# Input rows of a streaming-encoder step: load point, buffer of the sums of squares, and engine of the adds

## The chip, the core and the metric

One core of a Trainium2 chip runs the whole program. The metric is device time in microseconds (us), median of several executions; lower is better. The kernel before took 3329.35 us (median of 3 runs, 3321.38 to 3330.4). The engines are PE (TensorE, matmuls), PEld (its weight loads), DVE (VectorE), ACT (ScalarE), POOL (GpSimd) and SP (SyncE, which here issues most of the DMAs). Each engine works through its own list of instructions in order, and waits at the head of that list.

## What is computed

One inference step of a one-layer hybrid encoder on 2048 prompt frames, 16 meta tokens and 64 frames of a running stream, 2128 rows in all of 1024 features, in float32. Only its first stage is touched here:

```python
def rms_norm(x, g):
    y = x * rsqrt(mean(x * x, axis=-1) + EPS)
    return y * g

def input_projection(x, pos, lp):
    h = rms_norm(x, lp['attn_norm'])
    z = einsum('bld,dc->blc', h, lp['w_in'])      # 1024 -> 2728 columns
    q_lat, kv_lat, k_rope_raw, qkv, gate, beta_logit, a_logit = split(z)
```

After it come latent attention (8 heads), a gated delta rule with a causal convolution (4 heads), an output projection and a squared-ReLU MLP, each with residuals. They are the same in both kernels.

## The kernel before

The data are held transposed: features on the 128 partitions, rows along the free axis. The first stage, `phase_a`, splits the 2128 rows into five blocks of 336, 512, 512, 512 and 256 rows (`BLOCKS`), and the 2728 columns of the projection into 22 column tiles of 128 (the last, number 21, has 40). The column tiles are worked in batches: first tiles 21, 3 and 4 together, then tiles 5 to 16 singly (the convolution's inputs), then the rest. For each batch all five blocks are gone through. As the split rows of all blocks stay in SBUF, the input rows are loaded only once, in the first batch. This is where the change lies.

Every float32 product is made from three rounded ones: a value is split into a high part (ACT, L134) and a low part (DVE, L135), and PE adds high by high, low by high and high by low (L270, L271, L272). One column tile of one block (`col_product`) is 8 x 3 matmuls into one of six PSUM buffers.

`load_x(b)` takes the eight feature slices of a block's rows: SP issues the DMA of a slice into one of four buffers `x` (L224), ACT rounds it (L134), DVE subtracts (L135), ACT squares it (L227 for the first slice, L230 for the others), and DVE adds the squares up (L231) in the tile `ss`, of which there is one for all blocks (`bufs=1`). `mean_rstd` then sums `ss` over the partitions with a matmul by ones on PE (L241, two records), DVE scales (L243), and the reciprocal root is made on ACT (L141, L142) and DVE (L143 to L146) and put into `rstd[:, block]`, a tile as wide as all rows. `col_finish` multiplies a product by it (DVE, L282 for the tiles of the first batch), which frees the PSUM buffer. `finish_cols` squares the finished tiles 3 and 4 (ACT, L303), adds the squares on POOL (L307), and some column products later transposes tile 21 (PE, L317; copies on DVE, L318) and normalises tiles 3 and 4 (a second `mean_rstd`, then DVE L325) and writes them out.

`load_w` loads the weights of a column tile in two halves (SP, L256), scales them (DVE, L258) and splits them (L134, L135) into one of three buffers, so the first tile of the second batch can be split only when a tile of the first batch has been used for the last time.

The buffers `sq`, `nv`, `nt` and `nr` of these steps share four slots (`XTB`). The lists of the engines are drawn up before the run: instructions are taken in order of the program's text as far as their inputs and buffers are expected to be there, so a call that is moved forward in the text is given precedence over what now stands behind it.

## Time and profile before

| | before |
|---|---|
| median of the runs | 3329.35 us |
| lowest, highest | 3321.38, 3330.4 us |
| profiled execution, whole | 3322.66 us |
| its span, first to last instruction | 3320.9 us |
| mean granted TensorE clock | 0.979 |
| PE, DVE, ACT, POOL busy | 96%, 80%, 47%, 12% |

All durations below are from the profiled execution. Its span covers all but 1.8 us of it, and it lies 6.7 us under the median. A matmul's busy time is modelled and longer than the pace at which matmuls follow each other, so the pace is read from the starts of successive records, and a PE that is "busy" all the time says only that a matmul was always under way.

### The profile page before, as it was taken

The page shows a single profiled execution, that of the slowest core. Times are in us where ns is not written, and L with a number is a line of the kernel's source. Part 1 is how long each engine was busy: PE and PEld are TensorE (multiplying, and loading weights), DVE is VectorE, ACT ScalarE, POOL GpSimd, SP SyncE. Part 2 cuts the span into 40 slices and gives each one's busy share as a digit, 9 for nine tenths or more (in the row PEclk, how much of TensorE's full clock was granted, in tenths as well). Part 3 has the DMA queues.
Part 4 walks back from the last instruction along what each step waited for, and adds up shares of the span by engine and source line. Part 5 has one row for each costly group of instructions (what it writes and reads, how often), then busy time and mean ns, then how long its engine had stood idle before and what let it go on. Part 6 is the DMA issues. An engine that isn't in the chain of part 4 may idle for free.

```text
span 3320.9 us, 54512 instructions
## 1 busy us (share of the span) xinstructions
PE 3196.8 (96%) x20037; PEld 2943.1 (89%) x20037; DVE 2650.8 (80%) x5438; ACT 1558.4 (47%) x3495; POOL 400.5 (12%) x758
## 2 busy tenths in 40 slices
PE   9999998998979999999899999999999999999999
PEld 6888887888867778887799999999999999999999
DVE  8877654788758788888789888888888888988887
ACT  5555524555536868787564222334333333422232
POOL 0100013675510000000201000011000002100000
PEclk9999998999978999999999999999999999999999
DMA  4322213233221011010332222233222225122222
GB/s 132 91 74 70 74 63 100 87 104 100 59 57 35 20 34 34 25 37 26 106 99 75 77 77 75 76 110 109 88 76 73 65 73 160 58 73 77 77 74 70
DMA packets 318091, 248.09 MB, mean 75 GB/s; under 512 B 31776, under 2 KB 291616, under 8 KB 317760
## 3 DMA queue, kind: packets, MB, share of 16 engines
q1 hardware_dynamic: 300256, 219.21, 22.8%
q10 hardware_dynamic: 15536, 16.23, 1.6%
q0 software_dynamic: 2032, 9.18, 0.8%
q8 instruction: 157, 2.57, 0.3%
q14 instruction: 110, 0.90, 0.1%
HBM read 196.99 MB, written 47.52 MB: 74 GB/s over the span
## 4 chain that ended last, share of the span: by engine, by line
PE 83%; DVE 8%; ACT 2%; DMA 2%; issue 2%; POOL 1%; SPq 0%; POOLq 0%; DVEq 0%; ACTq 0%
PE psu L1601 23%; PE psd L1601 21%; PE ps L270 5%; PE ps L271 5%; PE ps L272 5%; PE pss L994 2%; PE pso L1011 2%; PE pss L995 2%; PE pss L996 2%; PE pso L1013 2%; PE pso L1012 2%; PE pspre L964 2%; DVE hl L1581 0%; PE psm L889 0%; DMA qh<-mrow 0%
## 5 line engine op out<-in xcount | busy, mean ns | idle before, releaser
L1601 PE MATMUL psu<-hh,uh 128*128 128x352 f32 x1728 | 563.0, 326 | 2.6 <-ACT uh L1497 2.1
L1601 PE MATMUL psu<-hl,uh 128*128 128x352 f32 x1728 | 557.3, 323 | 0.0
L1601 PE MATMUL psu<-hh,ul 128*128 128x352 f32 x1728 | 549.9, 323 | 0.0
L1601 PE MATMUL psd<-al,dh 128*128 128x352 f32 x1536 | 496.0, 323 | 3.5 <-DVE al L1790 3.2
L1601 PE MATMUL psd<-ah,dl 128*128 128x352 f32 x1536 | 494.6, 322 | 0.0
L1601 PE MATMUL psd<-ah,dh 128*128 128x352 f32 x1536 | 473.3, 324 | 11.1 <-DVE y L1709 7.4
L1709 DVE TENSOR_TENSOR y<-y,psd 128x352 f32<-128x352 f32 x768 | 386.6, 515 | 103.5 <-PE psd L1601 101.5
L1601 PEld LDWEIGHTS psu<-hh,uh 128*128 128x128 f32 x1728 | 325.7, 189 | 4.5 <-ACT uh L1497 2.5
L1601 PEld LDWEIGHTS psu<-hl,uh 128*128 128x128 f32 x1728 | 326.1, 189 | 1.2 <-issue 0.5
L1601 PEld LDWEIGHTS psu<-hh,ul 128*128 128x128 f32 x1728 | 323.9, 188 | 0.2 <-DVE ul L1475 0.2
L270 PE MATMUL ps<-hhi,whi 128*128 128x512 f32 (+5 forms) x880 | 313.6, 360 | 9.7 <-ACT hhi L134 7.1
L272 PE MATMUL ps<-hhi,wlo 128*128 128x512 f32 (+5 forms) x880 | 314.0, 358 | 0.0
L271 PE MATMUL ps<-hlo,whi 128*128 128x512 f32 (+5 forms) x880 | 312.5, 356 | 0.3 <-DVE hlo L135 0.2
L1601 PEld LDWEIGHTS psd<-ah,dh 128*128 128x128 f32 x1536 | 284.1, 188 | 16.9 <-DVE y L1709 11.5
L1601 PEld LDWEIGHTS psd<-al,dh 128*128 128x128 f32 x1536 | 289.1, 188 | 5.5 <-DVE al L1790 5.4
L1497 ACT CAST dh<-wr 128x512 fp32r<-128x512 f32 x192 | 119.3, 621 | 367.2 <-PE psd L1601 324.8
L1601 PEld LDWEIGHTS psd<-ah,dl 128*128 128x128 f32 x1536 | 288.8, 188 | 0.0
L1788 ACT CAST ah<-u 128x352 fp32r<-128x352 f32 x192 | 93.4, 487 | 398.6 <-DVE u L1786 280.0
L135 DVE TENSOR_TENSOR Pl<-P,Ph 128x512 fp32r<-128x512 f32 (+4 forms) x352 | 211.2, 611 | 52.2 <-ACT Ph L134 49.7
L998 ACT ACTIVATE P<-pss 128x512 f32<-128x512 f32 (+4 forms) x352 | 185.9, 539 | 87.6 <-PE pss L996 76.9
L965 DVE TENSOR_REDUCE mp<-pspre 128x1 f32<-128x296 f32 (+6 forms) x400 | 189.1, 500 | 31.1 <-PE pspre L964 29.2
L1714 POOL TENSOR_TENSOR y<-y,v 128x352 f32<-128x352 f32 x40 | 40.8, 1043 | 1330.8 <-DVE y L1709 1330.7
(458 smaller groups left out, 7266.5 us busy)
## 6 DMA issues: line engine op xcount, KB each, us to landing
wr<-in_w_up SPq DMA_DIRECT2D x192, 256.0 KB
wr<-in_w_down SPq DMA_DIRECT2D x192, 256.0 KB
qn<-scr_qN SPq DMA_DIRECT2D x32, 384.0 KB
wr<-in_w_out SPq DMA_DIRECT2D x48, 256.0 KB
wraw<-in_w_in SPq DMA_DIRECT2D x42, 256.0 KB
scr_convT<-s SPq DMA_DIRECT2D x36, 256.0 KB
mixr<-scr_mixT SPq DMA_DIRECT2D x12, 704.0 KB
out_y_T<-y SPq DMA_DIRECT2D x48, 176.0 KB
```

The lines of the kernel that those rows point to most:

```text
L135: (lo_eng or nc.vector).tensor_tensor(lo, src, hi.bitcast(F32), op=ALU.subtract)
L270: nc.tensor.matmul(ps[:m, :n], whi[:, k, :m], hi[:, k], start=k == 0, stop=False)
L271: nc.tensor.matmul(ps[:m, :n], whi[:, k, :m], lo[:, k], start=False, stop=False)
L272: nc.tensor.matmul(ps[:m, :n], wlo[:, k, :m], hi[:, k], start=False, stop=k == 7)
L964: nc.tensor.matmul(ps[:, :z - a], qh[:r, i * 128:(i + 1) * 128], kh[:r, a:z], start=True, stop=True)
L965: nc.vector.tensor_reduce(m[:, i:i + 1] if one else mp[:, j:j + 1], ps[:, :z - a], axis=AX.X, op=ALU.max)
L994: nc.tensor.matmul(ps[:w, off:], kh[:r, s:s + w], qh[:r, off:], start=True, stop=False)
L998: nc.scalar.activation(p[:w, off:], ps[:w, off:], AF.Exp)
L1497: self.nc.scalar.copy(t[0], src)
L1601: self.nc.tensor.matmul(ps, w, h, start=i == 0, stop=i == len(steps) - 1)
L1709: adds.append(nc.vector.tensor_tensor(Y[j][:, d], Y[j][:, d], ps, op=ALU.add).ins)
L1788: done = nc.scalar.copy(A[f, j][0], u).ins
```

## The change

Three edits, all in the first batch of `phase_a`:

1. `load_x` of the next block was called after the first of the three column products of a block. Now block 1 is loaded at that place within block 0, and block b+2 is loaded after the third column product of block b, ahead of `finish_cols(b)`.
2. The sums of squares are no longer gathered in the tile `ss`, but in the block's own columns of `rstd`, which `mean_rstd` reads and later overwrites with the result. The tile `ss` (512 float32 per partition) goes.
3. The seven adds of squares of each block (L231) are put on POOL.

```diff
                         new = n == 0 and ct == batch[0]
                         if new:
-                            self.mean_rstd(self.xss, BLOCKS[b][1] - BLOCKS[b][0], D, self.rstd[:, BLOCKS[b][0]:BLOCKS[b][1]])
+                            self.mean_rstd(self.rstd[:, BLOCKS[b][0]:BLOCKS[b][1]], BLOCKS[b][1] - BLOCKS[b][0], D, self.rstd[:, BLOCKS[b][0]:BLOCKS[b][1]])
                         zs.append(self.col_finish(ct, w[2], b, ps))
-                        if new and b + 1 < len(BLOCKS):
-                            self.load_x(b + 1)
+                        if new and b == 0:
+                            self.load_x(1)
                         wait -= 1
                         if wait == 0:
                             for _ in late:
                                 pass
+                    if n == 0 and b + 2 < len(BLOCKS):
+                        self.load_x(b + 2)
                     if min(batch) < 5 or 21 in batch:
...
-        ss = self.xp.tile([128, NB], F32, name="ss", tag="ss", bufs=1)
+        ss = self.rstd[:, b0:b1]
...
-            nc.vector.tensor_tensor(ss[:, :n], ss[:, :n], sq[:, :n], op=ALU.add)
-        self.xss = ss[:, :n]
+            nc.gpsimd.tensor_tensor(ss[:, :n], ss[:, :n], sq[:, :n], op=ALU.add)
```

## Rows read from the trace of the kernel before

**Rows 1.** The page, busy time and share of each engine over the whole span.
```profile
PE 3196.8 (96%) x20037; PEld 2943.1 (89%) x20037; DVE 2650.8 (80%) x5438; ACT 1558.4 (47%) x3495; POOL 400.5 (12%) x758
```
**Rows 2.** Windows: length, busy us (count) by engine, granted clock, DMA share, GB/s.
```profile
11.00:84.70 73.70, 73.70 (x349) 53.82 (x349) 61.56 (x120) 43.62 (x85) 4.11 (x3) 1.00 0.41 126
84.70:99.30 14.60, 11.20 (x56) 9.97 (x55) 14.18 (x30) 7.59 (x17) 1.30 (x1) 0.77 0.22 68
380.00:400.00 20.00, 20.00 (x106) 17.43 (x105) 11.68 (x22) 11.83 (x22) 0.00 (x0) 1.00 0.30 94
540.00:560.00 20.00, 11.24 (x61) 9.71 (x59) 14.22 (x30) 9.17 (x34) 13.04 (x21) 0.66 0.61 179
```
**Rows 3.** Waits of PE, 11 to 99.3 us, the longest: total us, times, longest.
```profile
PE ps L270 <- ACT whi L134: 2.1, 1, 2.1
```
**Rows 4.** Windows of PE alone: busy us (matmuls), granted clock, DMA share, GB/s.
```profile
84.90:90.30 5.40, 3.66 (x28) 1.00 0.26 73
93.10:99.10 6.00, 5.99 (x21) 0.50 0.25 87
```
**Rows 5.** Timeline of PE: start us, duration us, instruction, shape; pace is start to start.
```profile
24.02 0.32 PE L271 MATMUL ps<-hlo,whi 128*128 128x336 f32 x1
24.17 0.32 PE L272 MATMUL ps<-hhi,wlo 128*128 128x336 f32 x1
...
44.29 0.39 PE L271 MATMUL ps<-hlo,whi 128*128 128x512 f32 x1
44.52 0.39 PE L272 MATMUL ps<-hhi,wlo 128*128 128x512 f32 x1
...
75.69 0.38 PE L317 MATMUL ps<-ident,zt 40*128 40x40 f32 x3
...
82.38 0.28 PE L272 MATMUL ps<-hhi,wlo 128*128 128x256 f32 x1
82.50 0.28 PE L270 MATMUL ps<-hhi,whi 128*128 128x256 f32 x1
...
86.45 0.55 PE L270 MATMUL ps<-hhi,whi 128*40 128x256 f32 x3 [1.51 <-ACT hhi L134]
```
**Rows 6.** Waits of ACT, then of SP's DMA queue, 10 to 99 us.
```profile
ACT ss L227 <- PE ps_n L241: 10.8, 4, 4.3
...
SPq L224 <- ACT ss L227: 19.5, 4, 6.6
```
**Rows 7.** Timeline of SP and ACT around the last block's rows.
```profile
72.03 7.22 SPq L224 DMA_DIRECT2D x<-in_xT  x2
83.91 1.64 SPq L224 DMA_DIRECT2D x<-in_xT  x3
...
78.48 0.42 ACT L227 ACTIVATE ss<-x 128x256 f32<-128x256 f32 x1 [2.12 <-PE ps_n L241]
85.99 0.41 ACT L134 CAST hhi<-x 128x256 fp32r<-128x256 f32 x1 [0.98 <-DMA x<-in_xT]
89.89 1.14 ACT L134 CAST whi<-wraw 128x512 fp32r<-128x512 f32 x2 [1.20 <-PE ps L271]
```
**Rows 8.** Windows of line L231 alone, the adds of squares on DVE.
```profile
11.00:84.70 73.70, 16.89 (x27) 1.00 0.41 126
```
**Rows 9.** POOL by shape: a product of 512 columns, and the adds L307.
```profile
L638 POOL TENSOR_TENSOR o<-o,fr 128x512 f32<-128x512 f32 x16 | 16.6, 1041 | 0.6
L307 POOL TENSOR_TENSOR sq<-sq 128x512 f32<-128x512 f32 x9 | 13.7, 1520 | 104.0 <-ACT sq L303 103.8
```
**Rows 10.** Timeline of DVE and POOL, two places where both work at once.
```profile
48.18 0.42 DVE L145 TENSOR_SCALAR nt<-nt 128x512 f32<-128x512 f32 x1
...
57.92 1.26 POOL L307 TENSOR_TENSOR sq<-sq 128x512 f32<-128x512 f32 x1 [20.17 <-ACT sq L303]
58.21 0.31 DVE L318 COPY bt<-ps 128x8 f32<-128x8 f32 x3 [1.03 <-PE ps L317]
...
96.11 1.30 POOL L307 TENSOR_TENSOR sq<-sq 128x512 f32<-128x512 f32 x1 [15.07 <-ACT sq L303]
96.19 1.50 DVE L145 TENSOR_SCALAR nt<-nt 128x512 f32<-128x512 f32 x1
```
## What the change will do to the time

> **What bounds the kernel now.** I read the page first: PE is busy 96% of the span, DVE 80%, POOL 12% [rows 1]. A gain must therefore come from places where PE has nothing to do or runs slowly. So next I cut the first batch of `phase_a`, the only part that the edits touch, into windows [rows 2]. The reader is to see two stretches. From 11 to 84.7 us a matmul is always under way, at the full granted clock. From 84.7 to 99.3 us PE is busy 11.20 of 14.60 us, at a mean granted clock of 0.77. After that PE is full again, and the windows up to 540 us look like the one at 380 to 400 us, 20.00 of 20.00 busy at clock 1.00 [rows 2].
>
> PE's waits from 11 to 99.3 us name what it lacked: the longest is one of 2.1 us for weights at the start [rows 3], the next one of 1.5 us at 86.45 for the rounded rows of the last block [rows 5]; all others are shorter. The busy time hides part of the loss, so I count the matmuls against their pace. Successive starts are 0.23 us apart with 512 columns, 0.15 with 336 and 0.12 with 256 [rows 5].
> - 84.9 to 90.3 us, last block: 28 matmuls of 256 columns [rows 4] need 28 x 0.12 = 3.4 us; they took 5.4. Lost 2.0.
> - 90.3 to 93.1 us: four transposes, at 0.38 for three [rows 5] some 0.5 us; the stretch is 2.8. Lost 2.3. The next column tile's weights are not split yet.
> - 93.1 to 99.1 us: 21 matmuls of 336 columns [rows 4] need 21 x 0.155 = 3.3 us; they took 6.0, at a granted clock of 0.50, that is the 1.2 GHz level, after the idle time before. Lost 2.7.
>
> Together **7.0 us**, 0.21% of the time. This is all that PE can win back in this batch apart from the start.
>
> Why the last block is late is told by ACT's and SP's waits [rows 6]: four times ACT stood at L227, the first square of a block, until PE had read the one `ss` tile of the block before (10.8 us in all), and as ACT frees the four `x` buffers, SP stood with the next row DMAs behind it (19.5 us). For the last block that reads [rows 7]: ACT gets to L227 at 78.48, two row DMAs take SP from 72.03 to 79.25, the last three go out from 83.91 on, and ACT rounds a slice at 85.99, when PE is idle.
>
> **Part 1, the tile `ss` goes.** Every block writes its own columns of `rstd`, so L227 has nothing of another block to wait for. That removes four waits of ACT (10.8 us) and SP's behind them. Between 11 and 84.7 us PE was busy without a gap [rows 2], so the first three cost it nothing and what counts is the last one: its slices come at least the 2.1 us earlier that ACT waited at 78.48 [rows 7].
>
> **Part 2, one column product earlier.** Per block moved: 8 DMAs on SP, 16 instructions on ACT, 8 on DVE and 7 adds now precede the third of the block's finishing steps and the next block's first product, instead of standing behind it. One product of 24 matmuls of 512 columns is 24 x 0.23 = 5.5 us. With part 1 the last block's rows are 5.5 to 8 us earlier; they were late by less than 5.4 us, the length of the first lost stretch. So the 2.0 us go. Then tile 21 finishes its last block two products (2 x 24 x 0.12 = 5.8 us) before PE runs out, instead of all three tiles ending together as the slices trickle in; the next weights need 3.7 us from ACT's first rounding at 89.89 [rows 7] to PE's first product with them at 93.1 and a little more. They fit, so the 2.3 us go too, and with no idle time PE keeps its clock, so the 2.7 us go. If that cover fails (the split of the weights queued behind late DVE work), 2.3 + 2.7 = 5.0 us of the 7.0 stay.
>
> What the moved steps pass: on SP, the small writes of tile 21 and of tiles 3 and 4, for which nobody in this batch waits but the four spare buffers of their tiles; on ACT, the two squares of `finish_cols`; on POOL, the one add L307, now behind up to seven adds, some 7 x 1.04 = 7.3 us [rows 9]; its reader on PE, the second mean, comes three column products (16 us) later. All of it lies beside PE's work.
>
> **Part 3, the adds on POOL.** From 11 to 84.7 us 27 adds took 16.89 us of DVE [rows 8]; they go. On POOL an operation with two inputs of 512 columns takes 1.04 us alone [rows 9], so seven take 7.3 us, with contention (1.52 us, rows of L307 [rows 9]) 10.6 us, against a block's period of 72 x 0.23 = 16.6 us of products alone. POOL was busy 4.11 of 73.70 us [rows 2], so the sums are ready in time, and the squares' four slots come free at a pace that ACT can live with.
>
> But the adds do not leave DVE alone. At 96.11 an add runs on POOL, and DVE's L145, which takes 0.42 us at 48.18, takes 1.50: it was held 1.08 us [rows 10]. At 58.21 three copies out of PSUM take 0.31 us together inside an add of POOL: not held [rows 10]. So an add costs DVE between 0 and 1.08 us, by what DVE does next. DVE's other work in that stretch is 61.56 - 16.89 = 44.7 of 73.7 us, a share of 0.61, so I take 0.61 x 1.08 = 0.66 us per add: 27 x 0.66 = 17.8 us, as much as is freed. I expect DVE to stay as loaded as it is, 83%. Its room is the freed 16.9 and the idle 73.7 - 61.56 = 12.1, together 29.0 us, or 1.07 us per add; the upper bound of the hold uses it up exactly.
>
> The Trainium skill has a rule here, in "SBUF — State Buffer", section "Who interferes with whom": one pair of SBUF ports is shared by the two engines as an exclusive lock, and a DVE instruction with two SBUF inputs, or in a two-port mode, waits for a POOL instruction that reads SBUF to end. The trace agrees, with 1.08 us held against none for the copies out of PSUM. By that rule the subtractions of the low parts are held as well, which puts the hold near its upper bound; the sum would still be the same 7.0 us, with no slack left on DVE.
>
> Before 11 us, where PE waits 2.1 us for weights [rows 3], about three of the other eight adds leave DVE (16.89 / 27 = 0.63 us each) and as many holds come (0 to 1.08): between 3 x -0.63 = -1.9 and 3 x 0.45 = +1.4 us. I take 0, since that wait ends on ACT's rounding of the weights, which keeps its place, and keep both ends for the range.
>
> **Sum.** 7.0 us saved. Against the profiled execution: 3322.66 - 7.0 = 3315.7 us. That execution is 6.7 us under the median, so against the median 3329.35 - 7.0 = **3322 us**. PE is full for 440 us after this place, so the gain is handed on as a plain shift.
>
> **Rivals.**
> 1. *Half of it.* The rows come in time, but the weights' handover after the last block still stops PE, because DVE's list there still holds the reciprocal roots, L282 and the held steps. Then only the 2.0 us are won: 3327 us. For it: DVE is busy 14.18 of 14.60 us in that stretch [rows 2]. Against: the adds and subtractions of the last block, which are part of this, move away.
> 2. *The change does not do what it says.* The columns of `rstd` are one tile; if the squares of a block are made to wait for all uses of that tile, ACT waits as before, and the result is 3329 us. Against: at 86.45 PE starts on the last block half a microsecond after ACT began to round one slice of it at 85.99 [rows 5, 7], with other slices of the same tile still to come, so dependences follow the parts of a tile.
> 3. *More than PE's stall.* Where the second stage begins, PE is busy 11.24 of 20 us, at clock 0.66 [rows 2]. The 2 KB per partition that `ss` gives up moves the pools behind it, and which loads of the second stage must wait for which buffer of the first may change. If 5 of the 8.8 us without a matmul go as well: 3329.35 - 12 = 3317 us. Nothing shows that it will, and it could as well turn the other way.
> 4. *Slower: DVE becomes the bound.* If each add holds DVE for the 1.52 us that POOL needs under contention [rows 9] rather than 1.08, the 27 adds cost 41.0 us against room for 29.0: DVE is 12 us late at 84.7 us, PE waits for its subtractions and for PSUM buffers that L282 frees, and nothing of the 7.0 is won: 3329.35 + 12 = 3341 us. It decides from a mean hold of 1.07 us per add. For it: DVE was 84% busy there. Against: part of DVE's work reads PSUM and is not held, and a hold ends with POOL's use of the ports, 1.08 us in the row at hand. The page named above gives this rival its mechanism.
>
> **How the numbers follow.** Forecast 0.56, rival 1 0.14, rival 2 0.07, rival 3 0.12, rival 4 0.11. About 0.3% (10 us) is what a measurement of this kernel can tell from no change. The forecast, rivals 1 and 2 lie within it; but the runs of before themselves spread over 9 us, so of the forecast's 0.56 some 0.12 may be read as more than 10 us. Faster by over 0.3%: 0.12 + 0.12 = 0.24. Slower: 0.11. Within: 0.65. The range takes in the forecast with the start's bounds and the spread of the runs, and rivals 1 to 3: 3312 to 3335 us. Rival 4 lies outside it.
>
> **What would show it.** In the changed kernel's trace: no wait of ACT's first square for PE; SP's row DMAs all out before about 75 us; PE at clock 1.00 through the last block and the first block of the next column tile, with 28 matmuls of 256 columns there in about 3.4 us; the start of PE's first product of the second batch some 4.3 us earlier than 93.1, and everything after 7 us earlier; POOL with 35 adds of 1.0 to 1.5 us; DVE operations with two SBUF inputs stretched to about 1.7 us beside them, copies out of PSUM not. The prediction is wrong if PE shows new waits for DVE between 11 and 85 us, or if the stretch from 540 us on differs by more than the shift.

## The result, and the profile after

| | before | after |
|---|---|---|
| median of the runs | 3329.35 us | 3363.2 us (3360.59 to 3365.1, 3 runs) |
| ratio after / before | | 1.0117, 95% interval 1.0101 to 1.0133 |
| profiled execution, its span | 3322.66, 3320.9 us | 3360.59, 3358.6 us |
| mean granted TensorE clock | 0.979 | 0.973 |

The change makes the kernel 34 us slower. The forecast was 3322 us, the range ended at 3335. The page of the changed kernel gives the busy time of the engines, to be read against [rows 1]:

```profile
PE 3215.1 (96%) x20037; PEld 2955.3 (88%) x20037; DVE 2651.2 (79%) x5403; ACT 1556.0 (46%) x3495; POOL 453.7 (14%) x793
```

DVE has 35 instructions less and the same busy time, so what the adds freed was given back. In its trace line numbers are one or two higher than before (the adds are L233, the transposes L318, their copies L319). Next the windows of the changed kernel, as in [rows 2]:

```profile
11.00:84.70 73.70, 60.86 (x242) 40.66 (x243) 64.39 (x86) 41.45 (x81) 43.97 (x29) 0.86 0.42 123
84.70:99.30 14.60, 14.60 (x63) 10.67 (x60) 11.62 (x19) 5.11 (x11) 6.25 (x7) 1.00 0.15 50
...
40.00:60.00 20.00, 10.41 (x36) 5.45 (x36) 18.16 (x22) 10.05 (x19) 9.95 (x7) 0.66 0.34 98
```

Where PE was busy for 73.70 of 73.70 us, it now stands for 12.8 us, most of it between 40 and 60 us, and the clock falls with it (0.66 there). PE's waits from 11 to 110 us name the cause, against [rows 3]:

```profile
PE ps L318 <- DVE bt L319: 9.6, 1, 9.6
PE ps_n L242 <- POOL sq L308: 2.3, 1, 2.3
PE ps L272 <- DVE hlo L135: 0.5, 1, 0.5
```

PE stands once for 9.6 us between two transposes of tile 21, because DVE has not yet copied the first ones out. What DVE and POOL do in that time is in their timelines, POOL first:

```profile
23.43 26.01 POOL L233 TENSOR_TENSOR rstd<-rstd,sq 128x512 f32<-128x512 f32 x14 [8.04 <-ACT sq L232]
50.75 0.90 POOL L308 TENSOR_TENSOR sq<-sq 128x336 f32<-128x336 f32 x1 [1.30 <-ACT sq L304]
...
74.63 1.26 POOL L308 TENSOR_TENSOR sq<-sq 128x512 f32<-128x512 f32 x1 [2.27 <-ACT sq L304]
...
38.58 12.02 DVE L135 TENSOR_TENSOR hlo<-x,hhi 128x512 fp32r<-128x512 f32 x8 [1.63 <-ACT hhi L134]
50.52 0.68 DVE L244 TENSOR_SCALAR nv<-ps_n 128x512 f32<-128x512 f32 x1
51.12 1.07 DVE L135 TENSOR_TENSOR hlo<-x,hhi 128x512 fp32r<-128x512 f32 x1
52.12 0.29 DVE L319 COPY bt<-ps 64x8 f32<-64x8 f32 x3
...
41.13 1.63 POOL L233 TENSOR_TENSOR rstd<-rstd,sq 128x512 f32<-128x512 f32 x1
41.53 1.78 DVE L135 TENSOR_TENSOR hlo<-x,hhi 128x512 fp32r<-128x512 f32 x1
```

POOL makes 14 adds back to back, 1.86 us each on average instead of the 1.04 of [rows 9]; DVE makes the eight subtractions of the next block beside them, 12.02 us for eight, 1.50 each; and behind them stand the three copies for which PE waits. The two engines take turns, and neither reaches its pace alone: from 39.4 to 47.9 us one add and one subtraction start every 1.69 us (the last two lines are such a pair), about the sum of what the two take alone, 1.04 and 0.68 us.

The second stop of PE, 2.3 us up to 75.95, is for POOL's add L308. POOL itself had waited 2.27 us there for its input, a square that ACT made only at 73.93 us, behind squares and rounded rows of the next blocks. Behind each of the two stops PE runs at a low clock for some us (0.58 from 50 to 60 us, 0.77 from 70 to 80).

To see where the 38 us arise, equal instructions of PE are compared in the two traces. Five marks serve for every kernel below: the start of the last block's first product in the first batch (78.6 us before), the start of the second batch's first product (93.1), the start of the first stage's last product (538.7), the end of the gated delta rule's last product (950.0), the program's last product (3316.6). The table has the difference to the kernel before, and for the fourth mark what is lost between the third and the fourth alone.

All are from one profiled execution each. Executions of the same kernel differ (14 of the kernel before took 3323.53 to 3341.74 us), and the profiled one of the kernel before, 3322.66 us, is among the shortest, so differences of a few us at the last mark say little. At the last block the three kernels whose first batch is that of the kernel before stand at +0.4 to +1.9 us. The ratios are to runs of the kernel before made beside each kernel (their medians 3323.78 to 3331.92 us). Beside the single runs of the two kernels with extra operations on POOL, of x_late_transposes and of x_half_on_pool it took 3337.25 us in one run; beside x_after_copies_on_act and x_adds_on_dve_copies_on_act 3322.63.

| kernel | last block | 2nd batch | first stage | 539 to 950 | end | median, ratio to before |
|---|---|---|---|---|---|---|
| changed kernel | +21.0 | +16.7 | +12.6 | +17.7 | +37.6 | 3363.2, 1.0117 |
| x_pool_adds_alone | +11.6 | +10.9 | +8.2 | +6.4 | +18.8 | 3337.39, 1.0035 (1.0020 to 1.0051) |
| x_own_sums_alone | +1.6 | +1.4 | +1.6 | +25.6 | +34.0 | 3352.6, 1.0077 (1.0048 to 1.0105) |
| x_adds_on_dve | +2.1 | +2.1 | +0.4 | +26.3 | +29.0 | 3353.07, 1.0082 (1.0050 to 1.0115) |
| x_extra_pool_reads | +9.1 | +14.9 | +13.8 | +35.2 | +47.3 | one run, 3369.95 |
| x_extra_pool_writes | +0.7 | +1.9 | +3.4 | +24.9 | +25.6 | one run, 3348.32 |
| x_half_on_pool | +9.8 | +5.5 | +1.4 | +12.1 | +15.3 | one run, 3337.91 |
| x_late_transposes | +2.1 | -1.2 | +11.5 | +21.5 | +33.2 | one run, 3356.89 |
| x_after_copies_on_act | +20.4 | +16.0 | +14.4 | +7.1 | +22.1 | one run, 3345.12 |
| x_adds_on_dve_copies_on_act | +2.2 | -0.7 | -3.8 | +12.4 | +9.4 | one run, 3332.01 |
| x_before_tiny_matmul | +0.6 | +0.6 | -0.2 | +25.5 | +25.5 | 3348.41, 1.0064 (1.0043 to 1.0084) |
| x_before_one_matmul | +0.4 | +0.3 | +5.9 | +4.3 | +10.8 | one run, 3334.48 |
| x_before_four_matmuls | +1.9 | +1.8 | +10.1 | +27.3 | +45.0 | 3366.71, 1.0100 (1.0066 to 1.0134) |
| x_after_one_matmul | +20.6 | +16.3 | +13.1 | +4.1 | +18.9 | 3338.24, 1.0027 (1.0015 to 1.0040) |
| x_copies_on_act_four_matmuls | +1.5 | -1.3 | -1.0 | +33.7 | +32.8 | 3350.51, 1.0057 (1.0036 to 1.0077) |
| x_copies_on_act_one_matmul | +1.4 | -1.5 | -3.7 | +1.4 | +11.8 | 3330.63, 1.0014 (1.0000 to 1.0029) |
| x_copies_on_act_two_matmuls | +1.3 | -1.6 | -2.9 | +10.9 | +18.1 | one run, 3340.73 |

So the loss has two parts, and they have different causes: 12.6 us in the first stage, where the change lies, and 25 us in stages whose text did not change, 17.7 of them before 950 us. The first part is itself a difference: at the last block the changed kernel is 21.0 us behind, and 8.4 us come back within the next five products, at the very place from which the forecast drew its 7.0 us. 3.1 come back within the last block, 1.2 at the end of the batch, and 4.1 in the first products of the second batch, which the kernel before runs at its low clock [rows 4] and the changed kernel does not.

For the second part, PE's waits of the changed kernel from 800 to 1000 us show what is new there (first two lines). In the kernel before (last two lines) `uf` holds PE 1.3 us in all and `fr` not at all:

```profile
PE gpp L547 <- DVE uf L575: 5.4, 6, 1.3
PE gpp L490 <- DVE fr L635: 4.1, 3, 1.4
...
PE gpp L578 <- DVE uf L574: 0.9, 2, 0.7
PE gpp L549 <- DVE uf L574: 0.4, 1, 0.4
```

### The profile page after: what moved, and what is told of

Same layout as the page of the kernel before. It is cut to its first block, busy times and chain, and to the rows that moved or that the text cites. A ratio compares the mean times of both kernels' runs of the same rounds, so it can differ in the third digit from the quotient of the medians.

```text
span 3358.6 us, 54545 instructions
## 1 busy us (share of the span) xinstructions
PE 3215.1 (96%) x20037; PEld 2955.3 (88%) x20037; DVE 2651.2 (79%) x5403; ACT 1556.0 (46%) x3495; POOL 453.7 (14%) x793
## 4 chain that ended last, share of the span: by engine, by line
PE 83%; DVE 8%; ACT 3%; DMA 3%; issue 2%; POOL 1%; SPq 0%; POOLq 0%; DVEq 0%; ACTq 0%
PE psu L1602 23%; PE psd L1602 20%; PE ps L271 5%; PE ps L272 5%; PE ps L273 5%; PE pso L1012 2%; PE pss L995 2%; PE pso L1014 2%; PE pss L996 2%; PE pso L1013 2%; PE pss L997 2%; PE pspre L965 2%; PE gpp L499 1%; DMA qh<-mrow 1%; PE psm L890 0%
## 5 line engine op out<-in xcount | busy, mean ns | idle before, releaser
L271 PE MATMUL ps<-hhi,whi 128*128 128x512 f32 (+4 forms) x880 | 318.0, 362 | 6.5 <-ACT hhi L134 5.6
L272 PE MATMUL ps<-hlo,whi 128*128 128x512 f32 (+4 forms) x880 | 314.9, 358 | 0.8 <-DVE hlo L135 0.5
L273 PE MATMUL ps<-hhi,wlo 128*128 128x512 f32 (+4 forms) x880 | 314.3, 358 | 0.2 <-DVE wlo L135 0.2
L135 DVE TENSOR_TENSOR Pl<-P,Ph 128x512 fp32r<-128x512 f32 (+4 forms) x352 | 210.7, 611 | 51.3 <-ACT Ph L134 49.0
```

The source lines that it names most:

```text
L135: (lo_eng or nc.vector).tensor_tensor(lo, src, hi.bitcast(F32), op=ALU.subtract)
L271: nc.tensor.matmul(ps[:m, :n], whi[:, k, :m], hi[:, k], start=k == 0, stop=False)
L272: nc.tensor.matmul(ps[:m, :n], whi[:, k, :m], lo[:, k], start=False, stop=False)
L273: nc.tensor.matmul(ps[:m, :n], wlo[:, k, :m], hi[:, k], start=False, stop=k == 7)
```

## The experiments

The theories. *Port* (A in some expectations): POOL's adds read SBUF and hold DVE's operations with two inputs in SBUF. *Order* (C): the lists of the later stages, drawn up before the run, come out otherwise, whatever it was that shifted them; its rival is that an edit harms there by itself, through the room of `ss` or the place of its instructions. *Transposes* (E): the 7.0 us of the forecast fail to come because PE stands at the last block's transposes behind DVE's list, which is the forecast's rival 1.

### The parts one by one

The load point and the sums in `rstd`, without the move to POOL:

```diff
-            nc.gpsimd.tensor_tensor(ss[:, :n], ss[:, :n], sq[:, :n], op=ALU.add)
+            nc.vector.tensor_tensor(ss[:, :n], ss[:, :n], sq[:, :n], op=ALU.add)
```

> Parts 1 and 2 of the change, the adds of squares left on DVE. Theory A (the adds on POOL and DVE's two-input steps take turns, and that alone costs the first batch its 12.6 us): the last input product of the first stage ends some 7 us earlier than the 538.7 us of before, with no wait of PE for DVE or POOL between 11 and 85 us. Theory B (the earlier load itself does it, since its DVE steps now stand ahead of the reciprocal root of the block before): the first stage ends some 10 us later than before, whatever engine adds. Theory C, on the further 25 us that the changed kernel loses after 800 us (the lists of the later stages come out in another order, by chance of the planner): the later stages differ from before by some amount between -15 and +30 us that has nothing to do with the adds, so that the whole is between 3307 and 3352 us. If the adds on POOL cause the later loss too, the whole is near 3322 us.

The first stage ended within 0.4 us of the kernel before, so the 12.6 us need the adds on POOL. The whole was still 27 us slower (1.0082), all of it behind the first stage. At the end of the first stage nothing is seen of the forecast's 7.0 us, though the last block's rows were in time and 1.8 of the 2.0 us were won within that block (+2.1 us at its first product, +0.3 at its last). The timeline of PE at the end of the first batch has the same stop as before in another place:

```profile
91.92 0.25 PE L317 MATMUL ps<-ident,zt 40*128 40x40 f32 x1 [1.16 <-DVE zt L282]
92.52 0.25 PE L317 MATMUL ps<-ident,zt 40*128 40x40 f32 x1 [0.35 <-DVE zt L282]
93.11 0.25 PE L317 MATMUL ps<-ident,zt 40*128 40x40 f32 x1 [0.35 <-DVE zt L282]
94.99 0.25 PE L317 MATMUL ps<-ident,zt 40*128 40x40 f32 x1 [1.63 <-DVE bt L318]
95.18 0.45 PE L270 MATMUL ps<-hhi,whi 128*128 128x336 f32 x1
```

The transposes wait 3.5 us for the scaled tile (`zt`) and for copies (`bt`), both on DVE's list, which held the reciprocal roots and the next weights' low parts ahead of them. The first product of the second batch started at 95.2 us, not at 88.8. So this stop is 1.8 us longer than before, and the products behind it give 1.7 us back.

The adds on POOL alone, in the kernel before (L231):

```diff
-            nc.vector.tensor_tensor(ss[:, :n], ss[:, :n], sq[:, :n], op=ALU.add)
+            nc.gpsimd.tensor_tensor(ss[:, :n], ss[:, :n], sq[:, :n], op=ALU.add)
```

> Part 3 alone: the adds on POOL, the one tile for the sums and the place of the load as before. Theory A: the first stage ends 5 to 15 us later than the 538.7 us of before, DVE's low-part subtractions take about 1.5 us instead of 0.6 while POOL adds. Theory B: within 2 us of before. Theory C: the later stages differ from before by an amount that is not the 25 us of the changed kernel, since the lists differ again (PE's list is the same as before for longer, up to about 1.2 ms).

This edit alone costs 8.2 us by the end of the first stage. DVE's subtractions of the rows with 512 columns, from 5 to 100 us, show why; the first line is of the kernel before, the second of this one, the third of the changed kernel (count, busy us, mean ns):

```profile
L135 DVE TENSOR_TENSOR hlo<-x,hhi 128x512 fp32r<-128x512 f32 x24 | 16.1, 684 | 0.9 <-ACT hhi L134 0.8
...
L135 DVE TENSOR_TENSOR hlo<-x,hhi 128x512 fp32r<-128x512 f32 x24 | 23.6, 996 | 1.0 <-ACT hhi L134 1.0
...
L135 DVE TENSOR_TENSOR hlo<-x,hhi 128x512 fp32r<-128x512 f32 x24 | 26.2, 1132 | 2.0 <-ACT hhi L134 2.0
```

The sums in `rstd` alone:

```diff
-                            self.mean_rstd(self.xss, BLOCKS[b][1] - BLOCKS[b][0], D, self.rstd[:, BLOCKS[b][0]:BLOCKS[b][1]])
+                            self.mean_rstd(self.rstd[:, BLOCKS[b][0]:BLOCKS[b][1]], BLOCKS[b][1] - BLOCKS[b][0], D, self.rstd[:, BLOCKS[b][0]:BLOCKS[b][1]])
...
-        ss = self.xp.tile([128, NB], F32, name="ss", tag="ss", bufs=1)
+        ss = self.rstd[:, b0:b1]
...
-        self.xss = ss[:, :n]
```

> Part 1 alone: each block gathers its squares in its own columns, load place and adds as before. Theory A: no loss in the first batch; ACT no longer waits for PE at the first square, and the first stage ends 2 to 7 us earlier than 538.7 us. Theory B: as A, or no change, since the load stays where it was. Theory C: the later stages differ from before by an amount of their own, between -15 and +30 us; its PE list after the first stage is nearly that of the run with the adds on DVE, so the two should differ little there.

It moves the first stage by 1.6 us and the whole by 0.77%: 25.6 us come between 539 and 950 us, as in x_adds_on_dve. This edit alone is as dear as together with the load point.

It also shows what part 1 does by itself. No first square of ACT waits for PE any more, and yet the last block's rows come no earlier: the last three row DMAs go out at 85.71 us (83.91 before [rows 7]), and PE waits 1.6 us for the rounded rows (1.5 before). ACT now stands at the reciprocal root instead, for DVE:

```profile
84.75 0.63 ACT L141 ACTIVATE nt<-nv 128x512 f32<-128x512 f32 x1 [4.58 <-DVE nv L243]
...
85.71 1.72 SPq L224 DMA_DIRECT2D x<-in_xT  x3
```

### What holds DVE

The kernel before, with more operations on POOL: once 35 that read SBUF, once 70 that only write it. They are useless work, put behind each add of DVE on the square that nobody reads any more:

```diff
-            nc.vector.tensor_tensor(ss[:, :n], ss[:, :n], sq[:, :n], op=ALU.add)
+            nc.vector.tensor_tensor(ss[:, :n], ss[:, :n], sq[:, :n], op=ALU.add); nc.gpsimd.tensor_tensor(sq[:, :n], sq[:, :n], sq[:, :n], op=ALU.add)
```

> The kernel before with one more POOL operation behind each DVE add of squares: POOL adds the square to itself in place, an operation that reads SBUF and is needed for nothing (35 in all). DVE keeps its own 35 adds, so DVE is not relieved at all. Theory A (a POOL operation that reads SBUF and a DVE operation with two SBUF inputs exclude each other): DVE's subtractions L135 and adds L231 of 512 columns take 1.2 to 1.6 us on average instead of 0.68 in the first batch, and the first stage ends 12 to 30 us later than 538.7 us. If POOL is merely a slow adder and does not hold DVE: DVE's operations stay at 0.68 us and the first stage ends within 4 us of before.

In the other kernel two memsets stand in the place of the added operation:

```diff
-            nc.vector.tensor_tensor(ss[:, :n], ss[:, :n], sq[:, :n], op=ALU.add)
+            nc.vector.tensor_tensor(ss[:, :n], ss[:, :n], sq[:, :n], op=ALU.add); nc.gpsimd.memset(sq[:, :n], 0.0); nc.gpsimd.memset(sq[:, :n], 0.0)
```

> The same place, but POOL fills the square's buffer with zeros twice instead, which keeps POOL busy about as long (some 1 us) and reads nothing from SBUF. Theory A: DVE's operations with two SBUF inputs stay near 0.68 us (at most 0.8), and the first stage ends within 4 us of before. If any POOL work holds DVE, it looks like the run with the reads.

The groups by shape from 5 to 100 us, DVE's subtractions and POOL's added operation, first with the reads, then with the writes:

```profile
L135 DVE TENSOR_TENSOR hlo<-x,hhi 128x512 fp32r<-128x512 f32 x24 | 22.2, 946 | 0.0
L231 POOL TENSOR_TENSOR sq<-sq 128x512 f32<-128x512 f32 x21 | 30.0, 1432 | 35.1 <-DVE ss L231 29.8 <-ACT nt L141 2.4 <-DVE bt L318 1.6
...
L135 DVE TENSOR_TENSOR hlo<-x,hhi 128x512 fp32r<-128x512 f32 x24 | 16.2, 687 | 4.1 <-ACT hhi L134 3.9
L231 POOL MEMSET sq<- 128x512 f32 x42 | 22.2, 532 | 32.2 <-DVE ss L231 30.9
```

With the writes POOL was at work for 22.2 us, about what the 21 additions would take unheld (21 x 1.04 = 21.8), and DVE's subtraction kept its 687 ns; with the reads POOL took 30.0 us and the subtraction 946 ns, less than the 1.2 to 1.6 us expected. So it is POOL's reading that holds DVE, and the first stage paid for it: +13.8 us against +3.4, and +12.3 against -0.8 at 121 us of the kernel before, ahead of a stop near 410 us that both have (see below). The Trainium skill says so in "SBUF — State Buffer", section "Who interferes with whom": a DVE instruction with two SBUF inputs contends with a GpSimd instruction that reads SBUF, not with one that only writes it. The trace agrees.

The whole change with the adds of odd slices, 4 of the 7 in a block, on POOL:

```diff
-            nc.gpsimd.tensor_tensor(ss[:, :n], ss[:, :n], sq[:, :n], op=ALU.add)
+            (nc.gpsimd if k % 2 else nc.vector).tensor_tensor(ss[:, :n], ss[:, :n], sq[:, :n], op=ALU.add)
```

> The whole change, but only every second add (4 of 7 in a block) on POOL, the others on DVE. Theory A: half of the loss or a little more, so that the first stage ends 5 to 9 us later than 538.7 us (after: 12.6), and DVE's subtractions of 512 columns take 0.9 to 1.2 us on average. Theory B' (the adds on POOL cost only because the sums come too late for PE): with half the chain on POOL the loss is nearly gone, within 3 us of 539. The whole is not forecast: by theory C it hangs on the order of the later lists, which is a new one.

The second batch began 5.5 us later, and the subtraction took 864 ns, between none (684) and all (1132), as *port* has it. At the last block it was 9.8 us behind, the changed kernel 21.0. The first stage ended only 1.4 us late, less than the 5 to 9 us expected: 4.1 us came back in the first products of the second batch, where the kernel before runs at its low clock, as many as in the changed kernel (16.7 to 12.6).

### Why the 7 us did not come, and whether it is DVE's load or the place

The load point and own sums with adds on DVE, and the last steps of the last two blocks put off until the second batch has begun:

```diff
+                        if n == 1 and b == 0: [None for _ in late]
...
-                        late, wait = self.finish_cols(batch, zs, b), FD[b == len(BLOCKS) - 1]
+                        prev, late, wait = late, self.finish_cols(batch, zs, b), 99 if n == 0 and b > 2 else FD[b == len(BLOCKS) - 1]
...
+                        if n == 0 and b == 4: late = (y for g in (prev, late) for y in g)
```

> Parts 1 and 2 with the adds on DVE, and the late halves of finish_cols of the last two blocks (transposes, second mean, writes) put behind the first column product of the next batch instead of ahead of it. Theory E (with the rows in time, PE stands at the transposes, whose inputs DVE finishes too late; that is where the forecast's 7 us went): PE no longer waits 4.6 us for L282 and L318 at 91 to 95 us, keeps its clock, and the first product of the second batch starts at about 88 to 90 us instead of 95.2; the first stage ends 4 to 7 us earlier than with the adds on DVE alone (539.1 us), near 533 us. If something else holds PE there: within 2 us of 539.

The second batch started at 91.9 us, 3.3 us earlier than in x_adds_on_dve and 1.2 earlier than before: in the right direction, but short of the 88 to 90 expected. At the matmul that the kernel before starts at 98.8 us it was even 3.8 us ahead. Then the put-off steps stopped PE after all: two of its waits from 100 to 560 us, the first of them in the second batch:

```profile
PE ps L319 <- DVE zt L284: 5.4, 1, 5.4
PE ps L272 <- ACT whi L134: 4.4, 1, 4.4
```

The second is for weights that ACT splits at 414 us behind the gates' work, and x_before_four_matmuls has a like one of 5.0 us at 413 us, with nothing changed before it but four matmuls. With the low clock behind it, that makes the 6.7 us by which the first stage of x_before_four_matmuls is later than the 3.4 us expected of it. Seven of the kernels here lose 1.4 to 7.0 us at that place, the kernel before and the changed kernel nothing; no run isolates the cause.

Next, the copies out of the transposes on ACT, in the changed kernel and in x_adds_on_dve:

```diff
-                nc.vector.tensor_copy(self.bt[:C, CHUNKS.index(m), :], ps[:C, 32:40])
+                nc.scalar.copy(self.bt[:C, CHUNKS.index(m), :], ps[:C, 32:40])
```

> The whole change, and the copies out of the transposes (L319) go on ACT instead of DVE, in every block; nothing is left out. Two theories of what the adds on POOL cost in the first batch. Place: DVE's mean load is not the bound, the harm is that PE's transposes wait behind a row of held subtractions, because their copies stand behind these on DVE. Then PE's wait of 9.6 us for L319 is gone, the first product of the second batch starts at 99 to 103 us instead of 109.8 (93.1 in the kernel before), the subtractions L135 of 512 columns stay held at a mean of 1.0 us or more. Load: DVE as a whole is too late, and PE only shows it at the copies. Then PE waits about as long for DVE elsewhere (the low parts hlo, the PSUM buffers that the scaling frees), and the second batch starts at 106 us or later. After the first stage the lists are others again, so the end of the program says nothing of this: 0 to +30 us there.

*Place*, as put there, fell: PE's longest wait stayed, with another releaser (waits of PE, 11 to 110 us; then ACT's timeline up to the copies):

```profile
PE ps L318 <- ACT bt L319: 13.1, 2, 9.0
...
46.88 0.62 ACT L134 CAST hhi<-x 128x512 fp32r<-128x512 f32 x1 [0.52 <-DMA x<-in_xT]
47.40 0.63 ACT L229 ACTIVATE rstd<-x 128x512 f32<-128x512 f32 x1
47.94 0.47 ACT L304 ACTIVATE sq<-zt 128x336 f32<-128x336 f32 x1
48.75 0.62 ACT L134 CAST hhi<-x 128x512 fp32r<-128x512 f32 x1 [0.35 <-DMA x<-in_xT]
50.28 0.62 ACT L134 CAST hhi<-x 128x512 fp32r<-128x512 f32 x1 [0.91 <-DMA x<-in_xT]
...
52.28 0.26 ACT L319 COPY bt<-ps 64x8 f32<-64x8 f32 x3
```

On ACT, too, the copies stand behind the next block's rows. ACT waits for each row's DMA, the DMA for one of four `x` buffers, and the buffer for DVE's held subtraction (eight in 11.99 us again; SP's queue waits 10.4 us for them from 36 to 53 us). Neither theory had this right: it is not DVE's list alone, but the whole chain of the next block's rows, put ahead of the transposes by the earlier load point and slowed by the adds to 1.5 us a slice.

> The load point and the sums in rstd as in the change, the adds on DVE, and the copies out of the transposes on ACT instead of DVE; nothing is left out. If the 7.0 us of the forecast failed to come only because PE stands at the transposes of the last block behind DVE's list (3.5 us of waits for zt and bt at 91 to 95 us in the kernel with the copies on DVE), the part of 1.6 us for bt goes, and with a shorter pause some of the low clock: the second batch starts at 90 to 93 us instead of 95.2, and the first stage ends 1 to 5 us earlier than in the kernel before (538.7). If the pause is set by DVE's list whatever engine copies (the scaling L282 itself is late, and the next weights' low part), the second batch starts at 94 us or later. After the first stage the lists are others than those of the kernel before, so +20 to +30 us may be added there.

Without the adds on POOL the same move works: the second batch starts at 92.4 us, 2.8 us earlier than with the copies on DVE, and the first stage ends 3.8 us earlier than before. From the last block on it gains 6.0 us on the kernel before (+2.2 to -3.8). So the forecast's gain is real for most of its 7.0 us, once the copies are out of DVE's list, while 2.2 us were lost ahead of that block. Its windows, 11 to 84.7 and 84.7 to 99.3 us, stand against [rows 2].

```profile
11.00:84.70 73.70, 72.20 (x336) 53.46 (x337) 64.83 (x119) 47.89 (x107) 4.00 (x3) 1.00 0.44 132
84.70:99.30 14.60, 13.75 (x86) 12.20 (x86) 13.93 (x23) 5.87 (x15) 1.34 (x1) 1.00 0.35 108
```

In the second stretch PE does 86 matmuls instead of 56 and the clock is 1.00 instead of 0.77: the low clock is gone, 3.1 us between the second and the third mark (2.7 forecast). Of the waiting, 4.3 us forecast, 1.9 are won within the last block and 1.0 at the end of the batch; only 0.7 show at the second batch's start, since PE now stands for 1.5 us before 84.7 us, where it was full.

### Where the other 25 us come from

If the later lists are what counts, then an edit without any meaning must cost as much, and another must give it back. Each kernel has extra matmuls of `ones` with some columns of `rstd` in the fourth batch (in one run below, later), into a PSUM buffer that nobody reads. With 64 columns, once, in the kernel before:

```diff
+                if n == 3: d_ = self.aps.tile([128, NB], F32, name="ps_n", tag="psn", bufs=2); [nc.tensor.matmul(d_[:, :64], self.ones, self.rstd[:, :64], start=True, stop=True) for _ in range(1)]
```

> The kernel before with one needless matmul of 64 columns by ones on PE after the fourth batch (about 0.1 us of PE; its result is not used). It leaves the first batch alone, but PE's list after the first stage comes out different from before in 887 of 18336 places, from the same place on as with each block's own sums alone. Theory C (the loss after 800 us comes with the order of the later lists, and that order flips with any small shift): the first stage ends within 1 us of before, and 10 to 30 us are lost between 800 and 980 us, in all 3335 to 3355 us. Theory D (the later loss is caused by the change itself, by memory places or by POOL's adds): within 3 us of before.

One matmul, 0.33 us of PE, makes the kernel before 0.64% slower. Its first stage ends within 0.2 us; 25.5 us come between 539 and 950 us, as in x_own_sums_alone, with the same lines among PE's waits from 800 to 1000 us, here of x_before_tiny_matmul:

```profile
PE gpp L546 <- DVE uf L574: 6.1, 6, 1.3
PE gpp L489 <- DVE fr L634: 5.4, 4, 1.4
```

The same matmul with 512 columns four times (`[:, :512]`, `range(4)`), which makes PE's later list equal, place for place, to that of x_own_sums_alone:

> The kernel before with four needless matmuls of 512 columns by ones on PE after the fourth batch (4 x 0.86 = 3.4 us of PE). PE's list after the first stage is then the same, row for row, as with each block's own sums alone. Theory C: 3.4 us in the first stage, and the same loss after 800 us as there, 25 to 32 us: in all 3352 to 3362 us. Theory D: 3.4 us and nothing else, some 3327 us.

27.3 us against 25.6 in that stretch: the same list, the same loss, without any of the change. The total lies above the 3352 to 3362 us expected, by the stop at 413 us. And once with 512 columns in the changed kernel, whose later list then differs from that of the kernel before in 269 of 18,336 places:

> The changed kernel with one needless matmul of 512 columns by ones on PE after the fourth batch (0.9 us). PE's list after the first stage then differs from that of before in only 269 of 18336 places, while the changed kernel's own differs in 3108. Theory C: the 12.6 us of the first batch stay, the 25 us after 800 us go for the most part: 3335 to 3345 us, and a first stage that ends near 552 us. Theory D: as the changed kernel, 3364 us.

The changed kernel becomes 25 us faster by one useless matmul (3363.2 to 3338.24; ratio 1.0027 to the kernel before). Its first stage is as late as ever (+13.1), the stretch behind it costs 4.1 us instead of 17.7. What a list does to PE is seen in the window from 850 to 900 us, in the order before, x_before_tiny_matmul, changed kernel, x_after_one_matmul:

```profile
850.00:900.00 50.00, 45.97 (x536) 42.44 (x537) 37.32 (x83) 26.37 (x100) 28.48 (x50) 1.00 0.22 57
...
850.00:900.00 50.00, 41.98 (x405) 39.73 (x404) 27.89 (x59) 18.66 (x71) 21.21 (x36) 0.80 0.19 46
...
850.00:900.00 50.00, 43.15 (x456) 40.50 (x456) 32.53 (x70) 23.03 (x93) 24.14 (x39) 0.86 0.23 59
...
850.00:900.00 50.00, 44.39 (x525) 40.60 (x523) 37.96 (x82) 27.15 (x102) 28.92 (x51) 1.00 0.26 64
```

In 50 us PE gets through 536 and 525 matmuls with one kind of list and 405 and 456 with the other. The waits for `uf` and `fr` add up to only 9.5 to 11.5 us from 800 to 1000 us. The clock goes with them: in these four windows it is granted at 1.00 where the waits are missing and at 0.80 and 0.86 where they are there. Over the whole stretch between the third and the fourth mark, the same 3600 matmuls in the kernel before and in x_before_tiny_matmul, it reads

```profile
538.70:950.00 411.30, 357.12 (x3600) 0.94 0.32 88
...
538.50:975.20 436.70, 373.01 (x3600) 0.89 0.30 83
```

so of the 25.5 us PE stands for 9.5 (63.7 against 54.2 us without a matmul), and the rest are matmuls that run longer, at a mean clock of 0.89 instead of 0.94.

Then the order theory was tried on a kernel with the shorter first stage, x_adds_on_dve_copies_on_act with four such matmuls:

> Load point and sums in rstd as in the change, adds on DVE, copies out of the transposes on ACT, and four matmuls of 512 columns with ones and rstd after the fourth batch whose results nobody reads (4 x 0.23 = 0.9 us of PE). With them PE's list after the first stage stands at 615 of 18,336 places otherwise than in the kernel before (at 1,357 without them). Order theory: the +13 us that the same kernel without these matmuls lost between 800 and 980 us came with the order of its later lists; they shrink to -3 to +5 us, the first stage ends 2 to 4 us earlier than in the kernel before, and the end is -5 to +4 us: 3320 to 3332 us beside 3323 to 3330 of the kernel before. If the loss hangs on something else that these edits do (the place of the copies, the room of the tile that went), it stays: +8 to +14 us between 800 and 980 us, and an end of +6 us or more.

It lost 33.7 us, not up to 5. The first stage behaved, though the four matmuls took 3.4 us in it, not the 0.9 expected; the later list did harm again, with `uf` 6.4 and `fr` 5.5 us. So the count of places that differ is no measure of a list. A closer look at the lists gave one that separates them: how many places of PE's list (weight loads counted) lie from a chunk's product L572, of which DVE makes `uf`, to the next L546. They are the same in all lists for most of the 16 chunks; the tenth and eleventh differ:

```
kind 1  tenth 31, eleventh 24   before; x_pool_adds_alone; x_after_one_matmul
kind 2  tenth 27, eleventh 23 or 27   changed kernel; x_own_sums_alone; x_adds_on_dve;
        x_before_tiny_matmul; x_before_four_matmuls; x_half_on_pool;
        both kernels with extra operations on POOL; x_after_copies_on_act;
        x_adds_on_dve_copies_on_act; x_copies_on_act_four_matmuls
```

The traces show the same two kinds: for the tenth chunk, 13 matmuls on from the last of L572 comes the next of L546 in kind 1, and 1 or 5 on in kind 2. By this x_late_transposes is of kind 2 as well (5).

With that, three more kernels were chosen for kind 1 before they ran: one matmul of 512 columns in the kernel before, the same in x_adds_on_dve_copies_on_act, and there two of them in a later batch (`n == 16`):

> The kernel before, and one matmul of 512 columns with ones and rstd after the fourth batch whose result nobody reads (0.23 us of PE, more than twice the 64-column one that cost 25 us). Its later list is of the kind 31 and 24, like that of the kernel before without any. Order theory: no wait for uf of 1.3 us, 0 to +7 us between the first stage's end and 980 us, and an end of 0 to +8 us. If any matmul there does harm, by itself or by what it shifts, it costs at least the 25 us of the smaller one.

> Load point and sums in rstd as in the change, adds on DVE, copies out of the transposes on ACT, and one matmul of 512 columns with ones and rstd after the fourth batch, whose result nobody reads (0.23 us of PE). The later lists fall into two kinds by the number of places on PE from a chunk's product L572 to the next L546 for the tenth and eleventh of 16 chunks: 31 and 24 in the kernel before and in the two kernels that lost 4 and 6 us between the first stage's end and 980 us, 27 and 27 or 27 and 23 in all others, which lost 7 to 34 us there. This kernel has 31 and 24. Order theory: its first stage ends 3 to 4 us earlier than that of the kernel before, it loses 0 to 7 us until 980 us and shows no waits of 1.3 us for uf, and its end is -4 to +4 us from the kernel before. If the kind of list is no cause, it loses 12 us or more after the first stage, as with no matmul or with four, and its end is +8 us or more.

> Load point and sums in rstd as in the change, adds on DVE, copies out of the transposes on ACT, and two matmuls of 512 columns with ones and rstd within the batches of the last third of the first stage, whose results nobody reads (0.5 us of PE). Its later list is of the kind 31 and 24. Order theory: the first stage ends 3 to 4 us earlier than in the kernel before, 0 to +7 us are lost until 980 us, end -4 to +4 us. If the kind of list is no cause: 12 us or more after the first stage, end +8 us or more.

From 539 to 950 us the three lost 4.3, 1.4 and 10.9 us, and none has a wait of 1.3 us for `uf`. The third missed its 0 to 7 us. In all, the kernels of kind 1 lost 1.4 to 10.9 us there, those of kind 2 7.1 to 35.2: the kind decides most of it, though not all. Within kind 2 the three that lost least, 7.1 to 12.4 us, wait for `uf` 0.8 us at most, the others 1.3. The sharpest pair is 64 columns against 512 in the kernel before: the smaller addition costs 25.5 us, the larger 4.3, and both put the same number of instructions into PE's list, so its length is not the cause.

The ends missed. x_before_one_matmul lost 5.9 us in its first stage, with a wait of 3.4 us for weights at 408 us, and ends +10.8. x_copies_on_act_one_matmul is 5.6 us ahead of the kernel before at 900 us and 8.4 us behind at 1200 us, in the attention stage, so it ends +11.8 us in the profile and at 1.0014 of the time before; x_copies_on_act_two_matmuls, too, loses some 10 us there. Its windows there, kernel before first:

```profile
1160.00:1200.00 40.00, 37.52 (x155) 0.83 0.27 70
...
1160.00:1200.00 40.00, 34.24 (x129) 0.70 0.27 69
```

It is again a list in which PE stands more and runs slower, but no run isolates that one: it stays open. No kernel of these beat the kernel before.

## Why the prediction was wrong

**What bounds the kernel, and the 7.0 us** [rows 2 to 5]. The loss of 7.0 us at the end of the first batch was read rightly, and it can be won: the changed kernel gains 8.4 us from the last block on (+21.0 to +12.6). But PE comes there 21.0 us late and has no wait from 84.7 to 112 us, so this gain is no sign that the forecast's way to it was right. The loss of 21.0 us ahead of it is what the forecast put at nothing. Its own sign of being wrong came with it: PE's 9.6 us of waiting for DVE is new, and lies before 85 us.

Without that loss, in x_adds_on_dve, the 2.0 us of the rows came (1.8), and then PE stood at the transposes for DVE, which is the mechanism of rival 1. There the step "they fit, so the 2.3 us go too" of part 2 failed: it priced the weights' way over ACT and not the transposes' way over DVE, which was busy 14.18 of 14.60 us there [rows 2]. With the copies on ACT, 6.0 of the 7.0 us came.

Why the rows were late was read wrongly in part 1. The wait for the tile `ss` goes, as forecast, but x_own_sums_alone shows that the rows do not come the 2.1 us earlier that part 1 derives from it: ACT waits for DVE 4.6 us instead. They are in time only together with the load point, part 2 (x_adds_on_dve has no wait of PE for them); the load point without part 1 was not run.

**What the moved steps pass.** This is the step that failed in the first stage: "All of it lies beside PE's work". The forecast went through SP, ACT and POOL and left DVE out. There the eight subtractions of the next block now stand ahead of the transposes' copies. Unheld that would be 8 x 0.60 = 4.8 us; held it is 12.0 us, and PE stood 9.6 of them. Nor did the second mean's input come in time over ACT and POOL, though three products lie between: PE stood 2.3 us for L308. With the low clock behind it, the first stop puts the kernel 12.7 us further behind and the second 5.8, which is most of the 21.0 us. Neither part does all of it alone: at the last block the load point with the adds on DVE stands at +2.1 us, the adds on POOL with the old load point at +11.6.

**The hold per add.** The forecast took 0.66 us per add on average and an upper bound of 1.07 us from which DVE is the bound. The average was not far off. By the windows of line L135 alone, 11 to 84.7 us, kernel before and changed kernel (busy us of DVE and POOL, clock, DMA share, GB/s),

```profile
11.00:84.70 73.70, 22.31 (x37) 0.00 (x0) 1.00 0.41 126
...
11.00:84.70 73.70, 36.16 (x39) 0.00 (x0) 0.86 0.42 123
```

a subtraction takes 0.93 us instead of 0.60. All of DVE has 64.39 - (61.56 - 16.89) = 19.7 us more than it would have without the adds, 0.73 us for each of 27, and that with 86 instructions instead of 93 (with the seven missing ones taken out at the mean, an estimate, it is 0.85 us). So rival 4's point of 1.07 was not reached, and yet the kernel became slower by the hold, as rival 4 has it. That its 12 us are near the +12.6 at the end of the first stage is luck: it has nothing of the 7.0 us won, and in fact 21.0 were lost and 8.4 won back. What failed is the step from an average to a bound: "DVE's room" counted idle time over the whole stretch, while the adds come 14 in a row beside the subtractions behind which the copies stand that PE waits for, and there a subtraction takes 1.50 us. POOL's adds were mis-sized as well: 1.04 to 1.52 us forecast, 1.69 us on average and 1.86 in the row of 14.

**"The gain is handed on as a plain shift."** This is the larger error in the total: 25 of 38 us. From 100 to 540 us it holds, but not behind that. The later lists are made by expected times, and a matmul of 0.33 us is enough to make them fall otherwise. That the kernel before has a good one of these is not to be seen in its trace. Rival 3 had the idea that a later stage's start could turn "the other way", named memory as the cause and the place at 540 us, and gave it no price on the slower side. That memory is the cause is refuted as far as the lists go: x_before_four_matmuls gives back no tile and has the loss.

**Sum.** In the place of -7.0 us, 21.0 us lost and 8.4 won back in the first stage, +12.6; in the place of 0, 25 us behind it: 3322.66 + 37.6 = 3360.3 us, the profiled execution.

## What to carry to other kernels

Here DVE worked through a row of operations with two inputs in SBUF, and moving another such row to POOL freed nothing while the two overlapped (DVE busy 2650.8 us before, 2651.2 after). Where an edit does the like, count the longest overlapping row, not the average over a stage. When work is moved ahead in the text, go through every engine's list for what now waits behind it, first that of the engine with the least room (here DVE). Where lists are drawn up from expected times, an edit's own effect is read at the end of its own stage, and a useless small instruction put into the kernel before shows how much of a difference is only another list.

## What the hardware showed that was not expected

Two engines that hold each other did so in turns: with 14 adds in a row on POOL and eight subtractions on DVE, an add took 1.86 us and a subtraction 1.50 on average, against 1.04 and 0.68 us alone, and where they alternated strictly, one of each came every 1.69 us. POOL's memsets of the same size (532 ns, 42 of them) left DVE's subtraction at 687 ns.

Nine or ten waits of PE of up to 1.4 us within 200 us came with a granted clock of 0.80 and 0.86 in place of 1.00 from 850 to 900 us. In x_before_tiny_matmul they add up to 11.5 us, and the stretch from 539 to 950 us lost 25.5. The two do not always go together: x_copies_on_act_two_matmuls, without these waits, has 0.89 in that window.
